# The first tile's store in runs of 32 KB in place of 64 KB, in an RMSNorm-and-repeat kernel

## Chip, cores, metric

One core of a Trainium2 chip. The metric is the device time of one execution in microseconds (us). Times of different kernels are compared only over runs made on the same chip in the same rounds, and of the same (fast) state.

## The reference

```python
# x: (8, 512, 2048) float32, gamma: (2048,)
x_rep = np.repeat(x, 2, axis=1)
rms = np.sqrt((x_rep ** 2).mean(axis=-1, keepdims=True) + 1e-6)
return ((x_rep / rms) * gamma).astype(np.float32)   # (8, 1024, 2048)
```

33.6 MB are read and 67.1 MB are written, because each row is written twice.

## The kernel before

There are 8 tiles of 512 input rows. A partition holds 4 neighbouring input rows and, after the repeat, 8 neighbouring output rows: 64 KB that lie in one piece in SBUF and in the output. So a store of a tile is 128 runs of 64 KB, and a load is 128 runs of 32 KB. SP issues all of them from one queue; three tile buffers are in rotation.

Some words used below: a *run* is one contiguous piece that a DMA engine moves (a packet in the profile). A transfer is *issued* by an instruction on SP, its runs are *handed out* to the 16 engines (the generation of descriptors), and each engine reports when its share has *landed*. A transfer's *stage* is the time from the mean landing of the transfer ahead of it to its own.

```python
def store(i, k0, k1):
    nc.sync.dma_start(
        out=out_t[i, :, R * k0 * D : R * k1 * D],
        in_=ys[i][:, R * k0 : R * k1, :].rearrange("p j d -> p (j d)"),
    )
# ... (square, scale, repeat: see the whole kernel)
load(0, nc.sync, parts=2)
# ... (gamma is loaded on the ACT queue, and broadcast)
load(1, nc.sync)
load(2, nc.sync)
loads_after = {2: (3, 4, 5), 4: (6, 7)}
for i in range(ntiles):
    compute(i)
    store(i, 0, K)
    for j in loads_after.get(i, ()):
        load(j, nc.sync)
```

So the queue holds, in this order: loads 0, 1, 2; stores 0, 1, 2; loads 3, 4, 5; stores 3, 4; loads 6, 7; stores 5, 6, 7. I call each uninterrupted row of loads or stores a *group*, and the place where one kind follows the other a *passage*. There are five passages.

## Time and profile before

| | before |
|---|---|
| median (before the prediction, 3 runs) | 239.9 us (239.46 to 239.91) |
| span of the profiled run | 237.9 us |
| DVE busy, ACT busy | 41%, 42% |
| DMA packets of the SP queue | 2448, 98.5% of 16 engines' span |
| one store issue on SP | 332 to 366 ns |

DMA sets the end: both compute engines idle for more than half, and the DMA engines have work from 1.7 us on. The lines are in the prediction. The profile page counts packets and means. Where I give the spacing of runs or the time at which each of the 16 engines reports a transfer as done, it comes from the trace's packet and landing records, and I show it in a table.

### The profile page before, as it was taken

How to read it: one execution, taken by the hardware profiler on the slowest of the kernel's cores; microseconds unless marked ns; L12 is line 12 of the kernel's file. 1: busy time of each engine (PE TensorE's matmuls, PEld its weight loads, DVE VectorE, ACT ScalarE, POOL GpSimd, SP SyncE). 2: the span in 40 equal slices, each digit the busy share in tenths (PEclk: the TensorE clock that was granted, in tenths of full speed). 3: DMA queues.
4: the chain of work that ended last, by engine and by line, in shares of the span. 5: the costliest groups of instructions: out<-in, count | busy, mean ns of one | idle time of the engine just before them, and what ended most of it. 6: DMA issues, size and time to landing. Idle time of an engine off the chain costs nothing.

```text
span 237.9 us, 287 instructions
## 1 busy us (share of the span) xinstructions
DVE 96.5 (41%) x73; ACT 101.0 (42%) x106; POOL 2.5 (1%) x5
## 2 busy tenths in 40 slices
DVE  0049999960000000059999960000199990000000
ACT  2697999900000000099999920000599960000000
POOL 0030000000000000000000000000000000000000
DMA  7999998989899998999998999989998989999994
GB/s 265 436 446 441 441 441 353 530 353 496 386 452 430 397 485 353 441 441 441 441 518 364 464 419 430 452 369 430 435 518 364 518 364 485 397 452 430 408 474 176
DMA packets 2464, 100.69 MB, mean 423 GB/s; under 512 B 279, under 2 KB 285, under 8 KB 286
## 3 DMA queue, kind: packets, MB, share of 16 engines
q1 hardware_dynamic: 2448, 100.66, 98.5%
q14 instruction: 2, 0.02, 0.0%
q10 hardware_dynamic: 14, 0.01, 0.0%
HBM read 33.56 MB, written 67.11 MB: 423 GB/s over the span
## 4 chain that ended last, share of the span: by engine, by line
DMA 58%; ACT 12%; DVE 9%; issue 1%; POOLq 1%; ACTq 1%; SPq 0%
DMA y<-in_x_dram 33%; DMA out_dram<-y 21%; ACT sq L64 8%; DVE y L74 7%; DMA gamma_b<-in_gamma_dram 4%; ACT y L81 3%; DVE y L81 2%; ACT rms L68 1%; POOLq L136 1%; ACTq L95 1%; DVE rstd L73 0%; POOLq L96 0%; SPq L56 0%
## 5 line engine op out<-in xcount | busy, mean ns | idle before, releaser
L64 ACT ACTIVATE sq<-y 128x2048 f32<-128x2048 f32 x32 | 59.7, 1865 | 87.8 <-DMA y<-in_x_dram 87.8
L74 DVE SCALAR_TENSOR_TENSOR y<-y,rstd,gamma_b 128x2048 f32<-128x2048 f32 x32 | 75.3, 2352 | 4.1 <-POOL gamma_b L96 3.0
L73 DVE RECIPROCAL rstd<-rms 128x1 f32<-128x1 f32 x32 | 5.0, 158 | 94.6 <-ACT rms L68 94.3
L81 ACT COPY y<-y 128x4096 f32<-128x4096 f32 x8 | 28.7, 3590 | 1.4 <-DVE y L74 1.4
L81 DVE COPY y<-y 128x4096 f32<-128x4096 f32 x8 | 18.3, 2294 | 0.3
L68 ACT ACTIVATE rms<-ss,eps_t 128x1 f32<-128x1 f32 x32 | 9.4, 295 | 1.0
L64 ACT ACTIVATION_READ_ACCUMULATOR sq<-y 128x1 f32 x32 | 6.0, 187 | 0.0
L64 ACT ACT_TABLE_LOAD x1 | 1.3, 1283 | 3.0 <-issue 3.0
L96 POOL PARTITION_BROADCAST gamma_b<-gamma_b x1 | 2.3, 2294 | 12.2 <-DMA y<-in_x_dram 12.2
L68 ACT ACT_TABLE_LOAD x1 | 1.3, 1283 | 0.0
L98 DVE MEMSET eps_t<- 128x1 f32 x1 | 0.1, 59 | 0.8 <-PEq L125 0.8
L125 POOL MEMSET const-uint8-127<- 128x1 uint8 x1 | 0.1, 102 | 0.0
L125 POOL MEMSET const-bfloat16-1.0<- 128x1 bf16 x1 | 0.1, 101 | 0.0
L125 POOL MEMSET const-float32-0.0<- 128x1 f32 x1 | 0.1, 98 | 0.2 <-issue 0.2
L125 POOL MEMSET const-float32-1.0<- 128x1 f32 x1 | 0.1, 98 | 0.0
## 6 DMA issues: line engine op xcount, KB each, us to landing
y<-in_x_dram SPq DMA_DIRECT2D x7, 4096.0 KB, 14.6
y<-in_x_dram SPq DMA_DIRECT2D x2, 2048.0 KB, 7.4
out_dram<-y SPq DMA_DIRECT2D x8, 24.4
gamma_b<-in_gamma_dram ACTq DMA_DIRECT2D x6, 1.0 KB
gamma_b<-in_gamma_dram ACTq DMA_DIRECT2D x1, 2.0 KB
```

What stands on the lines that cost most here:

```text
L64: nc.scalar.activation(out=sq[:], in_=ys[i][:, K * (R - 1) + k, :], func=Act.Square, accum_out=ss[:])
L68: nc.scalar.activation(out=rms[:], in_=ss[:], func=Act.Sqrt, scale=inv_d, bias=eps_t[:])
L73: nc.vector.reciprocal(out=rstd[:], in_=rms[:])
L74: nc.vector.scalar_tensor_tensor(out=ys[i][:, R * k, :], in0=ys[i][:, K * (R - 1) + k, :], scalar=rstd[:], in1=gamma_b[:], op0=Alu.mult, o ...
L81: copy(out=y_r[:, k0:k1, 1, :], in_=y_r[:, k0:k1, 0, :])
L95: nc.scalar.dma_start(out=gamma_b[0:1, c0:c1], in_=gamma[c0:c1].partition_broadcast(1))
L96: nc.gpsimd.partition_broadcast(out_ap=gamma_b[:], in_ap=gamma_b[0:1, :])
L98: nc.vector.memset(eps_t, eps)
L125: nc = _bacc.Bacc("TRN2", target_bir_lowering=False, num_devices=1)
L136: with _tile.TileContext(nc) as tc:
```

## The change

Its intent is to write the first tile in smaller pieces. A limit on the last dimension of the transfer cuts each 64 KB run of the first store in two. The other stores keep their 64 KB.

```diff
     def store(i, k0, k1):
         nc.sync.dma_start(
+            max_dma_last_dim=4 * K * D * (1 if i == 0 else R),
             out=out_t[i, :, R * k0 * D : R * k1 * D],
             in_=ys[i][:, R * k0 : R * k1, :].rearrange("p j d -> p (j d)"),
         )
```

The order of instructions and their waits is the same on every engine; only the shape of the first store differs, 128 x 2 x 8192 in place of 128 x 16384.

## The prediction

> **What bounds the kernel now.** I read the page from its head down: first which engine is busy, then the slices, then the DMA queues, then the chain of waits, then who waits for whom on the issuing engine.
>
> ```profile
> DVE 96.5 (41%) x73; ACT 101.0 (42%) x106; POOL 2.5 (1%) x5
> ...
> DMA  7999998989899998999998999989998989999994
> ...
> q1 hardware_dynamic: 2448, 100.66, 98.5%
> ...
> HBM read 33.56 MB, written 67.11 MB: 423 GB/s over the span
> ```
>
> Both compute engines are idle more than half of the span. The row DMA gives the busy share of the 16 DMA engines in tenths: only the first and the last slice are really lower. The queue fed by SP holds 98.5% of the span in 2448 packets. Those are 896 load runs of 32 KB, 256 of 16 KB (tile 0 comes in two parts), 1024 store runs of 64 KB, and 272 semaphore writes of 4 bytes: 17 transfers on 16 engines each.
>
> ```profile
> DMA y<-in_x_dram 33%; DMA out_dram<-y 21%; ACT sq L64 8%; DVE y L74 7%; DMA gamma_b<-in_gamma_dram 4%; ACT y L81 3%; DVE y L81 2%; ACT rms L68 1%; POOLq L136 1%; ACTq L95 1%; DVE rstd L73 0%; POOLq L96 0%; SPq L56 0%
> ```
>
> In the chain of waits DMA leads with 58%. Its ACT and DVE pieces must not be read as work that sets the end: while they run, the DMA engines still have earlier transfers queued. The chain in order of time shows it for the transfer that the change touches:
>
> ```profile
> 24.69 2.30 DVE y L81
> 26.99 0.02 SPq L56
> 27.02 0.03 issue
> 27.05 25.77 DMA out_dram<-y
> ```
>
> The first tile's store is issued at 27.05 us and lands at 52.82, 25.77 us later, while 8.39 MB at full rate take 19.3. The difference is queueing behind the loads of tiles 1 and 2: the packet records have the last of tile 2's runs end at 32.4 to 33.0 us, and the store's first runs start then. So the DMA queue already has over 5 us of work when the store joins it.
>
> The packet records also give each engine's rhythm. I took the spacing of neighbouring runs on one engine: a 64 KB store run comes every 2.414 us, a 32 KB load run every 1.2094 us, a 16 KB load run every 0.6072 us. That is 27.1 GB/s per engine, or 434 GB/s for 16. One engine has 64 store runs, 56 load runs and 16 short load runs: 64 x 2.414 + 56 x 1.2094 + 16 x 0.6072 = 231.9 us of the 237.9 us span. The other 6 us are the start (the first run begins at 1.73 us, and the first two runs of each engine are together about 1 us slow), one stall of about 0.8 us told below, and the end (last landing 237.11 us). **The bound is the rate of each of the 16 DMA engines, busy from 1.7 us to the end.**
>
> **What the Trainium skill says.** The page "DMA: Bandwidth & Descriptors", section "Bandwidth" (Where 436 GB/s comes from), gives 435.2 GB/s as the ceiling of the 16 ports; the trace's 434 GB/s in the long stretches agrees. The same section (Why small descriptors are slow) gives about 3 cycles of fixed overhead per packet; at the 850 MHz named there, that is 3.5 ns, an estimate from that page. The trace has a duration for the same thing: two 32 KB runs take 2 x 1.2094 = 2.4188 us, one 64 KB run 2.414, so 4.8 ns for the extra one; two of 16 KB against one of 32 KB give 5.0 ns. The trace decides: 5 ns. The section "Why a DMA increments its semaphore by 16 and not by 1" says that the number of engines follows from the slowest dimension; that is 128 partitions before and after, and the 16 landings of every transfer agree for the kernel before. The page "Perfetto Trace Analysis", section "Per-instruction lifecycle", says that the time shown for a DMA issue is descriptor generation, not movement; the trace has 0.33 to 0.37 us for each store issue against some 25 us to its landing, which agrees.
>
> **The change part by part.** The order of instructions on every engine stays; only the first store's shape turns from 128 x 16384 to 128 x 2 x 8192. All waits are the same.
>
> It removes 128 runs of 64 KB and adds 256 of 32 KB, same bytes, same addresses, both contiguous in SBUF and in HBM. Per engine: 8 runs become 16, so 8 more run overheads. 8 x 4.8 ns = 0.04 us. This lies on the path, because the engines never drain until the end: everything behind the first store moves by 0.04 us. This is the one certain cost, 0.016% of the time.
>
> The issue of this one store may take longer. The issue of 128 runs takes 0.348 us; if generation scaled with runs it would be 0.7 us. But it would be done at 27.75 us, and the engines take up the store at 32.4 us: hidden, with 4.6 us to spare. The next thing SP does is the second store at 39.22 us: hidden too. Sum: +0.04 us.
>
> One thing could give time back. Just ahead of the first store, tile 2's last loads stall. Its last two runs per engine take up to 1.5 and 1.76 to 2.34 us where 1.213 is normal, on all 16 engines. The load's first landing comes 10.53 us after that of the load before it, where 9.71 is the rule: 0.82 us lost. The other two passages from load to store (near 118.5 and 176.5 us) cost 0.1 to 0.2 us. Which comes of the first store's run length, if any, no view tells.
>
> **The rivals.**
> *Nothing measurable (my choice).* Bytes, engines and queue order are the same, and the overhead is a tenth of the spread of the three runs (0.45 us). Time: 239.9 plus 0.04.
> *The stall at the first store shrinks.* For it: it sits on exactly the passage that the change touches, and it is larger than its two siblings, which shows something particular about the first passage. Against it: the siblings have 64 KB runs as well and stall little, so run length alone doesn't make it; and what is slow are load runs, before a store run is recorded. If all of the excess vanished, some 0.7 us: 239.2. I give a real gain of this kind 1 chance in 5.
> *More runs make it worse.* Twice as many descriptors are generated while loads are in flight. If the stall at 29 us is due to the generation at 27.05 us, it might double: +0.8 us, 240.7. For it: the stall begins 2 us after that issue. Against it: the issues of the second and third store at 39.22 and 51.39 us are followed by no such stall. 1 chance in 10.
> *A compute engine or a wait becomes the bound.* SP's loads of tiles 3 to 5 wait for the first three stores to land; were the first one late, load 3 would be issued late. But at 52.8 us the queue still holds two whole stores, till 91 us: 38 us of slack, hundreds of times the shift. I rule it out.
>
> **Range and chances.** The centre is 239.9 + 0.04 - 0.2 x 0.7 + 0.1 x 0.8, so 239.9 us. The three runs spread from 239.46 to 239.91; with the stall gone or doubled the time would be 239.2 or 240.7. A range of 239.2 to 240.5 us should hold it 8 times in 10. 2% is 4.8 us, six times the stall, and no part of the sum comes near: faster 0.01, same 0.98, slower 0.01.
>
> **What would show it right or wrong.** In the profile after: the SP queue has 2576 packets in place of 2448 (128 more), the same bytes; the first tile's runs come every 1.209 us; the first store, from its first run's start to its landing, takes 19.3 to 19.4 us; every later landing is moved by the same small amount, and the span is within 1 us of 237.9. SP issues the first store at 27.05 us within 0.1 us. If the stall between 29 and 33 us is gone, the first store lands near 52.0 in place of 52.8 and the end follows by as much: the second view was right. If the DMA rate during the first store falls visibly under 434 GB/s (32 KB stores having an overhead that 32 KB loads do not show), the step that took load runs as the measure of store runs was wrong; that would need 1 us per store to matter at all. A shift of several us would mean that the first store went to fewer engines or in another order, which would make this reading of the queue wrong.

## The result, and the profile after

| | before | after |
|---|---|---|
| median of 6 runs | 239.91 us (239.40 to 240.17) | 239.47 us (239.45 to 239.93) |
| ratio | | 0.9991, 95% interval 0.9977 to 1.0005 |
| span of the profiled run | 237.9 us | 237.7 us |

Ratios are the mean time of one kernel's fast runs over that of the other's fast runs of the same rounds, so they are not quite the ratio of the medians. The interval holds 1: no difference was measured. In microseconds it reaches from -0.55 to +0.12, and the +0.04 of the prediction lies in it.

The page of the kernel after, its lines on the slices, the SP queue, the bytes and the transfers' issues (KB each, us from issue to landing):

```profile
DMA  7999999999999898999999998989999999989894
...
q1 hardware_dynamic: 2576, 100.66, 98.7%
...
HBM read 33.56 MB, written 67.11 MB: 424 GB/s over the span
...
out_dram<-y SPq DMA_DIRECT2D x1, 8192.0 KB
```

The packets rose by 128, as one store with two runs per partition gives; the bytes are the same and the busy share nearly so (98.5% before). The chain in order of time, around the first store (start, us, what):

```profile
24.63 2.30 DVE y L82
26.94 0.02 SPq L56
26.96 0.03 issue
26.99 25.85 DMA out_dram<-y
52.84 0.02 issue
```

The store is issued at 26.99 us (27.05 before) and has landed at 52.84 us (52.82 before). Its issue took 402 ns where it took 348. The answers on the output tensor, first the kernel before, then the kernel after, give the least, median and greatest time of a store issue in ns:

```profile
L56 SPq DMA_DIRECT2D out_dram<-y x8: 332/343/366, 27.0 to 196.4; - x8
```

```profile
L56 SPq DMA_DIRECT2D out_dram<-y x8: 332/344/402, 27.0 to 196.2; - x8
```

The split costs the issuing engine 54 ns, and it had more than 12 us until its next issue. The 54 ns are not a price by the run: with 1024, 2048 and 4096 runs (experiments below) the issue of the first store took 402, 403 and 403 ns.

**Why the span fell by 0.2 us although the engines did not get faster.** Averaged over the 16 engines, the last store landed at 236.26 us before and at 236.44 after: later, not earlier. But the span ends with the slowest engine, and that was done at 237.11 us before and at 236.86 after. Between the two lies a chance that, as far as the records show, has nothing to do with the change: at 134.26 us (134.01 after) another queue fetches 8 KB of instructions, and the store run on the engine that it meets takes 2.77 us (2.86 after) in place of 2.418. Following the runs from end to start, I find that this fetch met, in the run before, the engine that ended last, its last run 0.56 us behind that of the second slowest; in the run after it met one that was not. The records don't name the engines, so this is a reconstruction, but the lengthened run is unambiguous. It accounts for the profiled pair; whether it also makes up the spread of the unprofiled runs was not tested.

### The profile page after: what moved, and what is told of

It reads as the page before. It is cut to its first block, busy times and chain, and to the rows that moved or that the text cites. A ratio compares the mean times of both kernels' runs of the same rounds, so it can differ in the third digit from the quotient of the medians.

```text
span 237.7 us, 287 instructions
## 1 busy us (share of the span) xinstructions
DVE 96.5 (41%) x73; ACT 101.0 (42%) x106; POOL 2.5 (1%) x5
## 4 chain that ended last, share of the span: by engine, by line
DMA 58%; ACT 12%; DVE 9%; issue 1%; POOLq 1%; ACTq 1%; SPq 0%
DMA y<-in_x_dram 33%; DMA out_dram<-y 21%; ACT sq L65 8%; DVE y L75 7%; DMA gamma_b<-in_gamma_dram 4%; ACT y L82 3%; DVE y L82 2%; ACT rms L69 1%; POOLq L137 1%; ACTq L96 1%; DVE rstd L74 0%; POOLq L97 0%; SPq L56 0%
```

## The experiments

The prediction left two questions: what does a run cost and does it lie on the path (8 runs more are too few to show in the whole time), and does the stall of tile 2's last loads, 0.8 us, come of the first store's run length?

**Theory A:** each extra run costs 4.5 to 5 ns on its engine, on the path, and nothing else changes. **Rival B:** the first store's run length is hidden. **Rival C:** the generation of descriptors becomes the limit. For the stall: **S1**, it comes of the store's run length; **S2**, of its issue; **S3**, of the passage itself; **S4**, it is the price of the first write to the output.

### Run length, one store and all stores

The first store in runs of 2 KB (e1), all stores in 32 KB (e2), all in 2 KB (e3):

```diff
+            max_dma_last_dim=2048 if i == 0 else 4 * K * D * R,   # e1
+            max_dma_last_dim=4 * K * D,                           # e2
+            max_dma_last_dim=2048,                                # e3
```

> First store alone in runs of 2 KB (32 per 64 KB row). Theory 'each extra run costs 4.8 to 5 ns on the path': 8 rows x 31 extra runs x 4.9 ns = 1.2 us more than the kernel before, in this store's stage (20.5 us in place of 19.3) and in the span. Rival 'the first store's run length is hidden behind other work': within 0.3 us of the kernel before. Rival 'descriptor generation becomes the limit': the issue of this store grows from 0.35 us towards 10 us, and the loss is more than 2 us.

> All eight stores in runs of 32 KB. Theory of 4.9 ns a run: 64 extra runs per engine, +0.31 us (ratio 1.0013). Rival 'run length also shortens the stalls where loads pass to stores': the three passages together give back some of it, at or under the kernel before. The stall of tile 2's last two load runs (29 to 33 us, 0.8 us) stays as it is if it doesn't come of run length.

> All eight stores in runs of 2 KB. Theory of 4.9 ns a run: 64 rows x 31 extra runs x 4.9 ns = 9.7 us per engine, all on the path: 249.6 us, faster/slower verdict slower by 4%. Rival 'hidden': within 1 us of the kernel before. Rival 'generation limits': more than 255 us.

| | median | ratio to before, 95% interval |
|---|---|---|
| before, same rounds | 239.34 us (9 runs) | |
| first store 2 KB | 241.65 us (4 runs) | 1.0092 (1.0078 to 1.0106) |
| all stores 32 KB | 239.63 us (5 runs) | 1.0015 (1.0002 to 1.0029) |
| all stores 2 KB | 257.34 us (4 runs) | 1.0752 (1.0733 to 1.0771) |

With all stores in 32 KB the cost is measurable: eight times the change gives +0.36 us (0.0015 x 239.5) with an interval of 0.05 to 0.7, where 0.31 was expected. Divided by eight, that is the 0.04 us of the prediction. The interval is wide; the trace is sharper: the six stores that are not followed by loads took 19.37 us on average in place of 19.34, some 4 ns for each extra run. B falls, and A holds for this size.

The first store in 2 KB costs 2.2 us where A expects 1.2. In the store's own stage A is right to the digit (table further down: 1.15 us). The rest comes later. Of rival C's two signs only the size of the loss came: this store's own issue took 403 ns and did not grow towards 10 us. But there is something new on the issuing engine. Its answer on the output tensor:

```profile
L56 SPq DMA_DIRECT2D out_dram<-y x8: 332/344/6650, 27.1 to 198.5; - x8
```

The 6650 ns are the issue of the *second* store, at 39.29 us. Its own 128 runs are the same as ever. It ended at 45.94 us, and in the kernel with all stores in 2 KB, where the second store has 32 times as many runs, it ended at 45.89. So the length of the hold-up comes from the store ahead: by the packet records, 89 of the first store's 256 runs per engine had not begun when it ended, in both kernels. My reading is that the runs ahead must all have been handed out first, and that there is room for only so many. The hold-up alone cost nothing: the second store's stage took 19.32 us (19.31 before).

With all stores in 2 KB the loss is 18.0 us where A gave 9.7, and over C's 255 us. The answer on the output tensor:

```profile
L56 SPq DMA_DIRECT2D out_dram<-y x8: 395/6310/15441, 27.0 to 207.8; - x8
```

A store that follows loads still takes 20.5 us (three of them: 20.53, 20.57, 20.53), as A says. One that follows another store takes 21.0 to 22.5 us, and its issue 5.9 to 15.4 us. That looks like C, the generation of descriptors as the limit. But the DMA engines show no idle time. Two stretches of this kernel, within its first and its third store:

```profile
36.00:50.00 14.00, 13.79 (x11) 11.99 (x13) 0.00 (x0) 1.00 1.05 409
76.00:90.00 14.00, 0.00 (x0) 0.00 (x0) 0.00 (x0) 1.00 1.03 386
```

(Columns: stretch, its length, busy time of DVE, ACT and POOL, clock, DMA share, GB/s. The share is over 1 because the records of neighbouring runs overlap: 0.084 us long, 0.080 apart.) The engines stay as busy while they move less: by the packet records a run takes 0.084 us in the first store and 0.089 on average in the third. And whenever one of the held-up issues ended, 80 to 98 runs per engine of the stores ahead had not begun, much as in the kernel with one 2 KB store. This speaks for issues that wait for the engines, not for engines that wait for the issues; C's number came, its reason is not shown. Why a 2 KB run takes longer behind another store of 2 KB runs stays open, and a wait inside the time of a run can't be seen in the records. That, and what is told of the passages below, makes up the rest of the 18 us.

To see where the second cost sets in, the first store alone in 8 KB and in 4 KB (the same edit with 8192 and 4096), and the 2 KB kernel once more:

> First store alone in runs of 8 KB: 8 rows x 7 extra runs x 4.7 ns = 0.26 us in its stage. The run with 2 KB lost 1.2 us in that stage as worked out, but some 1.1 us more at the later passages between stores and loads. If that second loss goes with the run count, a quarter of it comes here: about 0.5 us in all. If it needs the issue of the second store to be held up (6.65 us there, 0.34 before), it is absent here as long as that issue takes 0.34 us: about 0.26 us in all.

> First store alone in runs of 4 KB: 8 rows x 15 extra runs x 4.7 ns = 0.56 us in its stage (19.9 us in place of 19.35). If the second loss sets in where the second store's issue is held up, the two show together: issue of the second store over 1 us and a span about 1.6 us over the kernel before, or issue near 0.34 us and a span 0.6 us over it.

> The same kernel as the first store in 2 KB runs, profiled again. If the second loss of 1.1 us at the later passages belongs to the kernel, the span is 239.7 to 240.1 us again, with tile 5's load stage near 10.3 us. If it was chance, the span is near 238.8 us and that stage near 9.7.

Measured: 8 KB 239.78 us (4 runs), ratio 1.0006 (0.998 to 1.0031). 4 KB, one run, span 238.5 us. 2 KB again, one run, span 241.1 us, over the 239.7 to 240.1 expected. Tile 5's load stage took 10.28 us, 10.34 the first time: the second loss came again and belongs to the kernel. (The rest of the longer span is one engine that fell behind the others by over a microsecond; I did not pursue it.)

The first store's own stage, as the distance of the mean of 16 landings from that of the transfer ahead of it:

| first store in | extra runs per engine | its stage, us | more than before | per extra run | issue of the second store |
|---|---|---|---|---|---|
| 64 KB (before) | 0 | 19.38 | | | 0.34 us |
| 32 KB (after) | 8 | 19.41 | 0.03 | about 4 ns | 0.35 us |
| 8 KB | 56 | 19.63 | 0.25 | 4.5 ns | 0.35 us |
| 4 KB | 120 | 19.93 | 0.55 | 4.6 ns | 0.67 us |
| 2 KB | 248 | 20.53 | 1.15 | 4.6 ns | 6.65 us |

The stage repeats well: with 64 KB it took 19.37 to 19.38 us in four traces (before, and e4, e5 and e9 below, made on three chips), with 32 KB 19.41 and 19.42 in two (after and e2). So even the 0.03 us of the change itself can be seen there. The cost is linear in the number of runs from 8 KB to 2 KB, 4.6 ns each, where the load runs had given 4.8 to 5.0. The step of the prediction that read the price of a store run from load runs was right. Tile 5's load stage is 9.71 us with 8 KB (as before), 10.00 with 4 KB and 10.34 with 2 KB: the later loss grows as the second store's issue is held up, but the two were not separated by any run. With 2 KB the store just ahead of these loads is late as well (19.74 us where a store inside a group takes 19.31, and the loads win nothing of it back), so that passage costs 0.43 + 0.02 + 0.63 us by the landings. With the 1.15 of the first stage this is the 2.2 us measured.

### The stall

First S1. In the stretch from 28.9 to 32.3 us each engine begins the last two runs of tile 2's load. The answers for it, before and after, with the columns told above (in brackets the number of instructions):

```profile
28.90:32.30 3.40, 3.33 (x5) 3.33 (x7) 0.00 (x0) 1.00 0.99 308
```

```profile
28.90:32.30 3.40, 3.33 (x5) 3.33 (x7) 0.00 (x0) 1.00 0.99 308
```

These are two answers, equal to the digit. 308 GB/s over 3.4 us are 32 runs of 32 KB; the view counts a run, with its whole time, where it starts; a share of 0.99 of 16 engines over 3.4 us is 53.9 us of packet time, so 1.68 us a run where 1.21 is normal. The stall is there before and after, and the all-32-KB kernel shows 0.99 and 308 again. S1 has fallen.

Then the time at which the first store is issued. One try missed:

```diff
-        store(i, 0, K)
+        if i == 1:
+            store(0, 0, K)
+        if i > 0:
+            store(i, 0, K)                # e5
```

> First store issued after the second tile's compute (about 39.2 us in place of 27.05), so the DMA queue runs empty from about 32 to 39 us: some 7 us slower on purpose. Where does the stall of tile 2's last load runs go? If it is made by the first store's issue or its data following the loads, the last load runs take 1.21 us each, tile 2 lands at 31.9 to 32.5 us, and something of the stall may appear at 39 us. If it belongs to the loads or to that time, tile 2's last runs still take up to 2.3 us and land near 32.8 to 33.4.

The span was 238.0 us and the store was issued at 26.84 us, as ever. The edit moved a line of Python, not an instruction: SP has nothing to do but transfers, their order is the same, and each waits only for the buffers that it reads. The waits decide when a store goes out, not the place of its line among the compute. The run serves as one more profile of the kernel before.

Two that did move it: the first store in two transfers, of which the first is ready earlier (e6), and the second tile stored before the first (e7):

```diff
+        if i == 0:
+            store(i, 0, K // 2)
+            store(i, K // 2, K)           # e6
...
+        if i == 1:
+            store(1, 0, K)
+            store(0, 0, K)
+        elif i > 1:
+            store(i, 0, K)                # e7
```

> First store in two transfers: rows 0 and 1 of each group of four as soon as they are ready (issue near 23.4 us in place of 27), rows 2 and 3 at 27 us. Both still queue behind tile 2's loads, in runs of 32 KB. Theory 'the stall of tile 2's last loads is set off by the issue of the first store': it begins near 25.5 us in place of 29 us, on other runs of the loads. Theory 'it sits at the passage from loads to stores in the queue': it begins at 29 us again and the last two load runs are the slow ones. Time: within 0.5 us of the kernel before.

> The second tile is stored first: its store waits until 39.2 us, so no store is queued while tile 2's loads end and the DMA queue runs empty for some 7 us (what an earlier run was meant to do and did not, its program being the same as before on each engine). If the stall is a matter of a store standing behind the loads, tile 2's last runs take 1.21 us and tile 2 has landed by 32.5 us. If it belongs to the end of the loads themselves, the last runs are slow again and the landings lie at 32.7 to 33.4 us. Time: about 246 us.

With the halves, the first was issued at 23.21 us, and the stall began at 29.0 us again: tile 2's load took 10.67 us. S2 falls. With the second tile first, no store stood in the queue while tile 2's loads ended. The same stretch in this kernel, and the one after it:

```profile
28.90:32.30 3.40, 3.33 (x5) 3.33 (x7) 0.00 (x0) 1.00 0.72 309
```

```profile
32.50:39.30 6.80, 6.70 (x6) 6.77 (x5) 0.00 (x0) 1.00 0.00 0
```

Same runs, 0.72 in place of 0.99: 1.22 us a run, no stall, though the compute engines did the same work. Tile 2's load took 9.70 us. The second line shows the price, an empty queue until the store's issue at 39.06 us; the span was 247.0 us. So the loads themselves end without loss; it is the store standing behind them that makes them slow. S3 has its first support.

Is it the first write? A small extra store early, from the ACT queue (e4):

```diff
+    warm = singles.tile([P, D // 16], f32, name="warm")
+    nc.vector.memset(warm, 0.0)
+    nc.scalar.dma_start(out=out_t[7, :, 0 : D // 16], in_=warm[:])   # e4
```

> A small extra store (128 x 512 B of zeros to rows that the last store overwrites) goes out from the ACT queue at about 1 us. If the stall at 29 us is the price of the first write to the output, it is paid there or beside the start, tile 2's last runs are normal and the time falls by up to 0.8 us (ratio 0.997). If it is not, tile 2's load stage takes 10.55 us again in place of 9.71, and the time stays within 0.3 us of the kernel before or rises a little.

242.39 us (4 runs), ratio 1.0109 (1.0077 to 1.0140). Tile 2's load took 10.60 us: the stall is where it was, and S4 falls. The 2.6 us that the kernel lost are another thing. Who waited for whom on SP, of this kernel (us in total, times, longest):

```profile
SPq L52 <- DMA out_dram<-warm: 7.1, 1, 7.1
```

The transfers share eight semaphores in rotation. The extra store shifted the rotation by one, so tile 0's second load had to wait for the extra store (issued at 1.02 us, landed at 8.23) and went out at 8.25 us in place of 2.03. The engines ran dry, as the stretch from 8.0 to 9.2 us of this kernel shows:

```profile
8.00:9.20 1.20, 0.00 (x0) 0.85 (x1) 0.00 (x0) 1.00 0.00 1
```

Last, the pattern of all passages. With the mean landings, a load takes 9.71 us and a store 19.31 inside a group. How far the first and the last load of a group differ from that:

| load group | first load of the group | last load of the group |
|---|---|---|
| before: tiles 3 to 5; 6 and 7 | -0.31; -0.29 | +0.01; +0.01 |
| after: the same | -0.39; -0.27 | +0.07; +0.09 |
| first store 2 KB: tiles 3 to 5 | +0.02, again -0.04 | +0.63, again +0.57 |
| second tile first: tiles 3 to 5 | +0.18 | +0.72 |
| all 2 KB: the two groups | +0.14; +0.33 | +0.74; +0.80 |
| tiles 0 to 2, from an empty queue, 12 traces | | +0.76 to +1.08 |
| the same, no store behind (second tile first) | | -0.01 |

In all, of 26 load groups that followed stores, 21 began 0.26 to 0.49 us short, and those ended with -0.01 to +0.29; 5 did not begin short, and those ended with +0.57 to +0.80. A short beginning is no gain in itself: in the kernel before, the store just ahead of each such group took 19.63 and 19.60 us, late by about as much as the load is short. So the end of that load group in the 2 KB kernel looks like the end that every kernel but one has at tile 2, and the question becomes what makes a group begin short. This is a pattern over 26 groups, not yet a cause. One guess was that a store ahead in the same queue is enough (e9, the extra store on SP, behind tile 0's loads, so that nothing waits for it):

```diff
+    nc.sync.dma_start(out=out_t[7, :, 0 : D // 16], in_=warm[:])     # e9, behind load 0
```

> A small extra store (128 x 512 B of zeros to rows that the last store overwrites) stands in the SP queue between tile 0's loads and tile 1's load. In the runs so far, a group of loads that followed stores with its first load some 0.3 us short ended without a stall, and a group that began from an empty queue, or without that gain, lost 0.6 to 1.1 us at its end when stores stood behind it. If what matters is that a store went just ahead in the same queue, tile 1's load is about 0.3 us short, tile 2's load takes 9.7 us in place of 10.55, and the time falls by up to 0.8 us (ratio 0.9967 to 0.998). If the first passage stalls whatever went before, 10.5 us again and the time is the kernel before's plus 0.1 us. No extra wait as in the run with the ACT queue: tile 0's second load is still issued at 2 us.

239.83 us (5 runs) against 239.43 (9 runs), ratio 1.0013 (1.0000 to 1.0027). Tile 1's load was 0.04 us short, not 0.3, and tile 2's took 10.59 us. The guess fell; the pattern held once more. No version was found that gets the 0.8 us back, so none beats both kernels.

**What stays open:** why 2 KB runs grow longer when a store of 2 KB runs follows another, what inside the DMA engines links a group's beginning to its end, and why the 2 KB first store, whose runs are all done by 54 us, spoils the passage from stores to loads at 92 us. The held-up issue of the second store goes along with it (0.35, 0.67, 6.65 us) but no run takes one without the other.

## Why the prediction was right

- *The bound is the rate of each DMA engine.* Right. The losses above are found as longer stages or a dry spell of the DMA queue; the mean length of each kind of ACT and DVE instruction is the same in all traces within 5 ns.
- *+0.04 us from 8 more runs per engine at 4.8 ns.* Right within what can be measured: 4.6 ns per run from the shorter runs, +0.36 us (expected 0.31) from eight times the change. The stage itself rose by 0.03 us, and the runs in it came every 1.209 to 1.210 us, as named.
- *A longer issue is hidden.* Right, and smaller than the worst case allowed for: 54 ns in place of up to 350, and the same for sixteen times as many runs.
- *The stall might shrink, 1 chance in 5, or double, 1 in 10.* Neither: 10.58 us before, 10.55 after. The argument against it, that its siblings have 64 KB runs and hardly stall, was sound. That something is particular about the first passage was sound as well; as far as the pattern goes, it is that its loads started from an empty queue. The 0.1 to 0.2 us given for the two later passages hold for some engines only: by the mean landings their last loads lose 0.01 us.
- *More runs make it worse.* Not at this size, but the thought had something in it: at 2 KB the loss is about twice what the run price gives. It appears at later passages, not at the stall that was named.
- *Every later landing moves by the same small amount.* Only roughly: the mean landing moved by 0.04 us at the first store and by 0.18 at the last, the rest from the passages. This was taken for exact where it has a scatter of 0.1 us.
- *The first store takes 19.3 to 19.4 us from its first run's start to its landing.* Mis-sized, as it left out the time from the end of the last run to the landing, some 0.35 us: by that measure it took 19.72 us before and 19.75 after. From landing to landing it fits.
- *The span within 1 us of 237.9.* Right; but the sign of the difference, -0.2, was set by which engine an instruction fetch met, a term that the sum did not have.

## What to carry to other kernels

When the DMA queue never runs dry, price a change of run length as (extra runs per engine) x (nanoseconds per run), read from the spacing of neighbouring runs of different sizes; if that is under a tenth of the spread of the runs, predict no change, and prove the price with a kernel that makes many times as many runs. Look at what the issuing engine does as well: from some number of runs on (here between 64 and 128 per engine), the next issue is held up. A long issue alone does not show that the engines wait for it, so look at their busy share too. And losses can appear far from the transfer that was changed. And before you read a gain of 0.1% from two profiles, compare the mean of the engines' last landings with the slowest one.

## What the Trainium skill lacked or had wrong

- "DMA: Bandwidth & Descriptors", section "Bandwidth" (Why small descriptors are slow): 3 cycles a packet, 3.5 ns by my estimate from that page, are of the right size for runs of 2 to 64 KB too; the runs show 4.6 ns.
- The same page has nothing on how many runs can be queued before the next issue is held up: with 4096 runs of 2 KB ahead the second store's issue took 6.65 us in place of 0.34; with 2048 of 4 KB, 0.67; with 1024 of 8 KB, 0.35. When the held-up issue ended, 82 (4 KB) to 89 (2 KB) runs per engine of the store ahead had not begun.
- No page that I read tells that loads can slow down when stores stand behind them in the same queue: the last two load runs per engine of the first group took 1.68 us on average in place of 1.22, 0.76 to 1.08 us in all over 12 traces, and not when no store stood behind. Most later groups (21 of 26) did not lose this.
- "Perfetto Trace Analysis", section "Per-instruction lifecycle", fits in that the issue window leaves out the movement of the data: issue times of 0.33 to 0.40 us beside some 25 us to landing. That the window ends when all descriptors have been generated does not fit what the runs show: the first store's issue took 0.40 us with 256 runs and with 4096 alike, and it was the next issue that was held up for 6.65 us. The page speaks of a descriptor buffer that may be full, but gives no size. That most of the 6.65 us is waiting is my reading; the trace does not split it.
